# Last S5 layer: input product in float32, TensorE order written out, gate weight parts issued after the GELUs

## The chip, the cores and the metric

The kernel runs on one core of one Trainium2 chip. The metric is the device time of one execution, in microseconds, as the median of several runs. The engines are named as in the profile: PE is TensorE (matmuls and transposes), PEld its weight loads, DVE is VectorE, ACT is ScalarE, POOL is GpSimd, SP is SyncE. SP, ACT and POOL also issue DMA transfers, each in the order of its own queue.

## The reference

A residual trunk of four layers over 256 tokens of width 1024, all in float32. Each layer has a token mixer (layers 0 and 3 are S5, layer 1 is an attention, layer 2 a gated linear attention), a squared-ReLU MLP and a gated per-layer embedding. The change touches the S5 mixer of layer 3 alone:

```python
def s5_mixer(xn, w_in, ...):
    u = xn @ w_in                                  # 256 x 1024 times 1024 x 1024
    # per group of 16 channels: 64 complex states, a decayed scan over time
    x_re, x_im = einsum(u_blk, bbar_re), einsum(u_blk, bbar_im)
    s_re, s_im = associative_scan(...)             # in chunks of the sequence
    y = einsum(s_re, c_re) - einsum(s_im, c_im) + d_skip * u
    z1, z2 = split(gelu(y) @ w_glu, 2)             # 1024 x 2048
    return (z1 * sigmoid(z2)) @ w_out              # 1024 x 1024
...
h = h + s5_mixer(rmsnorm(h), ...)
...
h = h + (p[i] @ W_pp) * sigmoid(rmsnorm(h) @ W_pg)
```

## The kernel before

Activations lie transposed in SBUF: four tiles of 128 x 2 x 256 hold the residual stream. Almost every dense product is made of float32r matmuls on split operands. `parts` (lines 174 to 185) takes a raw weight tile of 128 x 1024, lets ACT cast it to a high part `whi` (L179) and lets DVE subtract that from the raw tile to get a low part `wlo` (L181). `scaled` (L363, L364) does the same with the activations. `col` (L198 to L200) then issues three matmuls for each 128 x 128 block of weights: high by high, high by low, low by high. Layer 0's S5 does not do so for its input product: there (L1158) the raw float32 weights are multiplied with the float32 activations, one matmul instruction per block, which the trace shows as two records.

The S5 layer works on four blocks b of 256 channels. Its steps have one-letter names, and a string of such steps (`FIRST` for layer 0, `LATER` for layer 3) is the order in which they are recorded:

- `D` loads a 512 x 256 piece of `w_in`, `h` splits it, `w` multiplies it (two pieces per block; pieces 2b and 2b+1 belong to block b and to the first and second half of the inputs). `c` scales the activations and squares them, `n` and `z` make the norm's factor (L330, POOL's power at L341, L351).
- `u` (L1166, DVE) scales the product and starts eight small DMAs that rearrange it into the tile `U` (L984), half issued by SP and half by ACT.
- `f` and `q` fetch the matrices that were prepared earlier for this block (`kept`, by POOL's queue). The first one that `f` fetches, `win`, has one buffer for all blocks.
- `x` is the way into the states (L996, 64 records on PE, written to two PSUM banks `wk`), `s` and `e` are the scan on DVE (L1006 to L1030), `y` is the way out (L1042) and the GELU on ACT (L1051).
- `t` transposes the block on PE (L1058) and copies it on ACT (L1059), `g` subtracts for the low part on DVE (L1231).
- `P` and `p` load and multiply the embedding's projection for the end of the layer (L446, float32 as it is).
- `d` loads a tile of the gate's half of `w_glu`, `l` splits it, `a` and `b` multiply it for the two column blocks of the gate (24 matmuls of `col` for each block of channels), with the sigmoid (L1257) after the last.

After these steps come the other half of `w_glu` and `w_out` as ordinary dense products, which wait for nothing but weights.

A tracing layer then places the instructions: it keeps each engine's program in an order of its own choosing that respects the data and the buffers, and need not follow the string. `in_order(engine)` (line 113) adds dependences that fix an engine to the recorded order; `issue_after` puts instructions behind a given one. In the kernel before, layer 3's steps have neither. Raw weight tiles share three buffers, the high and low parts four each, and every transfer waits in its issuing queue until its buffer is free.

What ends before layer 3's input product can begin is the product of the embedding's gate of layer 2 (`ple_gate`), whose last eight tiles use all high and low buffers, and whose results go through DVE and ACT (L468 to L471) into the residual stream that the S5 layer reads.

Of the kernel before, what the change touches and what calls it, by code (L numbers as in the profile page):

```python
# [12 lines left out]
AF = mybir.ActivationFunctionType  # L13
# [4 lines left out]
T, D, FF, DEPTH = 256, 1024, 4096, 4  # L18
# [12 lines left out]
d2 d3 t1 f3 x3 p2 p3 s2 a0 e2 y2 g1 q3 l2 d4 l3 d5 t2 b0 s3 a1 b1 g2 l4 e3 y3 l5 d6 d7 a2 b2 l6 l7 t3 g3 a3 b3"""  # L31

# [28 lines left out]
class Trunk:  # L61
# [373 lines left out]
    def plain_ple_proj(self, l, raws):  # L435

        nc = self.nc
        out = self.pp_done[l] = []
        for raw in raws:
            t = self.t4("pp", (128, 2, 2, T))  # L440
            for i in range(2):
                ps = self.psum((128, 2, T))
                for n in range(2):
                    for k in range(2):
                        c = (2 * i + n) * 128
                        nc.tensor.matmul(ps[:, n], raw[:, k, c:c + 128], self.praw[:, k], start=k == 0, stop=k == 1)  # L446
                nc.scalar.copy(t[:, i], ps)
                out.append(t[:, i])
                yield
# [583 lines left out]
    def s5_outputs(self, U, terms, out, tm):  # L1033

        nc = self.nc

        py = self.psum((128, 8, 64), "mk")
        gs = [slice(g * 64, (g + 1) * 64) for g in range(2)]
        def add(x, w, start=False, stop=False):
            for p in range(8):  # L1040
                for g in range(2):
                    nc.tensor.matmul(py[gs[g], p, :], x[gs[g], p, :], w[gs[g], :, p] if w is not tm else w[gs[g], p], start=start and p == 0,  # L1042
                                     stop=stop and p == 7, skip_group_check=True)
# [7 lines left out]
        nc.scalar.activation(G, py.rearrange("x p (i c) -> x i p c", i=4), AF.Gelu_apprx_tanh)  # L1051
        return G

    def s5_turn_over(self, G, hi):
# [55 lines left out]
    def s5_start(self, l):  # L1110


        nc, A = self.nc, self.A
        j = l // 3
        first = self.kept is None
# [29 lines left out]
        def product(i, between):  # L1145
            b, i = i // 2, i % 2
            if i == 0:
                us[b] = self.psum((128, 2, T), "acc")
            ps = us[b]
            if first:  # L1150
                raw = halves[2 * b + i]
            else:
                hi, lo = units.pop(("h", 2 * b + i))
            for n in range(2):
                c = slice(n * 128, (n + 1) * 128)
                for k in range(4):
                    if first:
                        nc.tensor.matmul(ps[:, n], raw[:, k, c], x[4 * i + k], start=i == k == n == 0, stop=i == 1 and k == 3, skip_group_check=True)  # L1158
                    else:
# [100 lines left out]
        steps = dict(D=D, h=h, w=w, u=u, c=c, n=n, z=z, f=f, j=j_, q=q_, r=r, i=i, o=o, k=k, x=x_, s=s, e=e, y=y, t=t, g=g, P=P, p=p, d=d, l=ahead, a=lambda b: gate(0, b),  # L1260
                     b=lambda b: gate(1, b))

        def run(order):
# [2 lines left out]
            return gT, v.get("last")  # L1266

        self.sg = []
        if first:
            halves = [self.raw0] + [self.half(w_in, i) for i in range(1, 8)]  # L1270
            x = [self.t4("x", (128, 4, T), tag="x4") for _ in range(2)]
            x = [x[k // 4][:, k % 4] for k in range(8)]
            scalars, v["ms"] = self.s5_scalars(j), self.psum((128, 2))

            def scaled(k):
# [170 lines left out]
```

## Time and profile before

| | |
|---|---|
| median of 3 runs | 1442.95 us (1440.83 to 1443.87) |
| profiled execution | 1441.32 us, its span 1439.3 us |
| granted TensorE clock, mean | 0.993 |
| PE busy | 1396.7 us, 97% of the span |
| DVE, ACT, POOL busy | 1047.1, 719.5 and 100.6 us |
| HBM traffic | 174 GB/s over the span |

The profile comes from one execution, 1.63 us below the median; about 2.0 us of its time lie outside the span. Times in the text count from the start of the span. Matmuls overlap: a record of 0.28 us can be followed by the next after 0.12 us, so costs in a row are taken from starts to starts.

### The profile page before, as it was taken

What the parts mean: (1) busy time and instruction counts of PE and PEld (TensorE: products, weight loads), DVE (VectorE), ACT (ScalarE), POOL (GpSimd) and SP (SyncE); (2) the same over time, 40 slices, a digit from 0 to 9 for tenths busy, and PEclk for the clock granted to TensorE, in tenths of its full rate; (3) what the DMA queues carried; (4) which work ended last, traced back from release to release, by engine and by line L of the source; (5) the groups of instructions that cost most, each with busy time, mean ns of one, the idle gap of its engine ahead of it and who ended that gap; (6) DMA issues with size and microseconds to landing.
All of it is one profiled execution on the core that took longest, in us unless ns stands there. A gap on an engine that the chain in (4) does not pass through costs nothing.

```text
span 1439.3 us, 26706 instructions
## 1 busy us (share of the span) xinstructions
PE 1396.7 (97%) x10818; PEld 1261.1 (88%) x10818; DVE 1047.1 (73%) x1652; ACT 719.5 (50%) x1118; POOL 100.6 (7%) x167
## 2 busy tenths in 40 slices
PE   9989999999999999999999999999997899999997
PEld 8888988889999888889988598888997799888897
DVE  9885678776866688897667468787676946766765
ACT  3233565454654655455567355445462345545543
POOL 3000000010010000000004000000003100000020
PEclk9999999999999999999999999999999999999999
DMA  9443656657554456766555256566656546556651
GB/s 297 111 120 108 180 171 196 189 183 238 171 157 136 122 167 193 248 226 211 196 161 170 94 153 196 195 215 197 205 162 210 172 152 181 179 183 194 188 189 59
DMA packets 143227, 254.54 MB, mean 177 GB/s; under 512 B 21648, under 2 KB 32240, under 8 KB 143104
## 3 DMA queue, kind: packets, MB, share of 16 engines
q1 hardware_dynamic: 129856, 227.66, 51.0%
q0 software_dynamic: 7360, 23.73, 4.8%
q10 hardware_dynamic: 5888, 1.44, 0.5%
q8 instruction: 84, 1.38, 0.4%
q14 instruction: 39, 0.32, 0.1%
HBM read 242.15 MB, written 7.86 MB: 174 GB/s over the span
## 4 chain that ended last, share of the span: by engine, by line
PE 63%; DMA 2%; DVE 2%; ACT 2%; issue 0%; DVEq 0%; POOLq 0%; ACTq 0%; SPq 0%
PE wk L234 9%; PE acc L234 7%; PE wk L236 4%; PE wk L198 4%; PE wk L199 4%; PE wk L200 4%; PE acc L198 4%; PE acc L199 3%; PE acc L200 3%; PE acc L236 3%; PE mk L234 3%; PE po L234 2%; PE mk L236 1%; PE acc L259 1%; PE acc L258 1%; PE acc L260 1%
## 5 line engine op out<-in xcount | busy, mean ns | idle before, releaser
L181 DVE TENSOR_TENSOR wlo<-raw,whi 128x1024 fp32r<-128x1024 f32 x404 | 492.0, 1226 | 276.2 <-ACT whi L179 274.6
L179 ACT CAST whi<-raw 128x1024 fp32r<-128x1024 f32 x404 | 420.8, 1049 | 489.4 <-DMA raw<-mlp_w 73.9
L234 PE MATMUL wk<-x,whi 128*128 128x512 f32 x576 | 181.3, 396 | 1.1 <-DVE relu L245 1.1
L236 PEld LDWEIGHTS wk<-x,wlo 128*128 128x128 f32 x576 | 106.8, 188 | 23.4
L234 PE MATMUL acc<-s,whi 128*128 128x512 f32 x384 | 119.2, 395 | 0.0
L236 PE MATMUL wk<-x,wlo 128*128 128x256 f32 x576 | 112.9, 279 | 0.0
L198 PE MATMUL acc<-x,whi 128*128 128x256 f32 x352 | 99.8, 287 | 1.8 <-DVE u L1166 1.0
L200 PE MATMUL acc<-x,wlo 128*128 128x256 f32 x352 | 99.9, 286 | 0.8 <-DVE wlo L181 0.8
L199 PE MATMUL acc<-x,whi 128*128 128x256 f32 x352 | 99.4, 285 | 0.0
L234 PEld LDWEIGHTS wk<-x,whi 128*128 128x128 f32 x576 | 90.3, 189 | 3.6 <-DVE relu L245 1.4
L236 PEld LDWEIGHTS acc<-s,wlo 128*128 128x128 f32 x384 | 71.0, 188 | 16.1
L234 PE MATMUL mk<-x,whi 128*128 128x512 f32 x256 | 81.5, 395 | 0.5 <-ACT whi L179 0.5
L236 PE MATMUL acc<-s,wlo 128*128 128x256 f32 x384 | 75.4, 280 | 0.0
L200 PE MATMUL wk<-s,wlo 128*128 128x256 f32 x256 | 72.4, 283 | 0.0
L199 PE MATMUL wk<-s,whi 128*128 128x256 f32 x256 | 72.4, 283 | 0.0
L198 PE MATMUL wk<-s,whi 128*128 128x256 f32 x256 | 72.4, 283 | 0.0
L198 PEld LDWEIGHTS acc<-x,whi 128*128 128x128 f32 x352 | 66.9, 191 | 3.3 <-issue 1.8
L200 PEld LDWEIGHTS acc<-x,wlo 128*128 128x128 f32 x352 | 67.2, 191 | 1.6 <-DVE wlo L181 1.3
L199 PEld LDWEIGHTS acc<-x,whi 128*128 128x128 f32 x352 | 67.2, 192 | 0.2
L234 PE MATMUL po<-s,whi 128*128 128x512 f32 x192 | 60.3, 395 | 0.0
L234 PEld LDWEIGHTS acc<-s,whi 128*128 128x128 f32 x384 | 59.1, 188 | 0.9
L234 PE MATMUL wk<-s,whi 128*128 128x512 f32 x192 | 59.1, 395 | 0.0
(404 smaller groups left out, 3362.9 us busy)
## 6 DMA issues: line engine op xcount, KB each, us to landing
raw<-mlp_w SPq DMA_DIRECT2D x256, 512.0 KB, 4.1
raw<-s_w_glu SPq DMA_DIRECT2D x32, 512.0 KB, 4.2
raw<-ple_gate SPq DMA_DIRECT2D x32, 512.0 KB, 3.6
raw<-fox_w_in SPq DMA_DIRECT2D x24, 512.0 KB, 3.8
raw<-gla_w_in SPq DMA_DIRECT2D x24, 512.0 KB, 4.6
raw<-s_w_out SPq DMA_DIRECT2D x16, 512.0 KB, 3.4
kept<-kept POOLq DMA_DIRECT2D x12, 512.0 KB, 4.7
raw<-s_w_in SPq DMA_DIRECT2D x11, 512.0 KB, 4.2
```

Of the source, the lines that this page charges most:

```text
L179: nc.scalar.copy(hi, raw)
L181: self.last_lo = nc.vector.tensor_tensor(lo, raw, hi.bitcast(F32), ALU.subtract)
L198: mm(ps, hi, x[:, 0], start=first, stop=False, skip_group_check=True)
L199: mm(ps, hi, x[:, 1], start=False, stop=False, skip_group_check=True)
L200: self.last_mm = mm(ps, lo, x[:, 0], start=False, stop=last, skip_group_check=True)
L234: mm(ps[n], hi[:, i, s], v[i], start=first and i == 0, stop=False, skip_group_check=True)
L236: self.last_mm = mm(ps[n][:, 0], lo[:, i, s], v[i][:, 0], start=False, stop=last and i == UK - 1, skip_group_check=True)
L258: mm(ps[half], a[:, 0, t], hi[:, k], start=k0 + k == 0, stop=False)
L259: mm(ps[half], a[:, 0, t], lo[:, k], start=False, stop=False)
L260: mm(ps[half], a[:, 1, t], hi[:, k], start=False, stop=k0 + k == nk - 1)
```

## The change

Layer 3 now makes its input product as layer 0 does. `D` loads the raw pieces with `half`, which places them in turn in buffers of the raw, the high and the low parts; step `h` is gone; `c` scales the activations in ACT alone, without a low part; `w` issues 8 float32 matmul instructions per piece where 24 float32r ones stood. `LATER` is written anew, without the `h` steps, with the products `w` spread between the steps of the blocks and `t3` between two gate products. The layer's steps stand under `in_order` for PE. The splits of the gate's weights (`l`) are issued after the last GELU recorded so far. The other lines only hand references on.

```diff
-LATER = """D0 D1 D2 h0 D3 h1 D4 c0 w0 h2 D5 n0 z0 f0 q0 w1 h3 D6 z1 h4 D7 w2 w3 u0 h5 P0 u1 h6 d0 x0 w4 h7 d1 w5 f1 q1 s0 x1 u2 w6 e0 y0 w7 f2 t0 l0 P1 s1 x2 q2 u3 p0 p1 e1 y1 g0 l1
...
+LATER = """D0 D2 D1 D3 c0 w0 w2 n0 z0 f0 q0 w1 z1 D4 D5 u0 w3 P0 u1 w4 D6 D7 d0 x0 s0 w5 d1 f1 q1 x1 e0 w6 y0 u2 s1 w7 t0 l0 g0 f2 x2 u3 P1 e1 q2 y1 l1 d2
...
     def s5(self, l):
...
-        with nullcontext():
-            steps = self.s5_start(l)
-            with nullcontext():
-                gT, last = steps()
+        steps = self.s5_start(l)
+        with nullcontext() if l == 0 else self.in_order(E.PE):
+            gT, last = steps()
...
         def D(i):
-            units["h", i] = self.raw(w_in[i % 2 * 512:(i % 2 + 1) * 512, i // 2 * 256:(i // 2 + 1) * 256], 4, 256)
-
-        def h(i):
-            units["h", i] = self.parts(units["h", i])
+            units["h", i] = self.half(w_in, i)
...
                 for k in range(4):
-                    if first:
-                        nc.tensor.matmul(ps[:, n], raw[:, k, c], x[4 * i + k], start=i == k == n == 0, stop=i == 1 and k == 3, skip_group_check=True)
-                    else:
-                        self.col(ps[:, n], v["x"][2 * i + k // 2][:, k % 2], hi[:, k, c], lo[:, k, c], i == k == n == 0, i == 1 and k == 3)
+                    self.last_mm = nc.tensor.matmul(ps[:, n], raw[:, k, c], x[4 * i + k], start=i == k == n == 0, stop=i == 1 and k == 3, skip_group_check=True)
...
         def c(_):
-            v["x"] = self.scaled(l)
+            for k in range(8):
+                nc.scalar.activation(x[k], self.H[k], AF.Identity, scale=self.gains[:, l, k:k + 1])
             v["sq"] = self.squares()
...
         def ahead(i):
-            units[i % 2, i // 2] = self.parts(units[i % 2, i // 2])
+
+            with nullcontext() if first else self.tc.issue_after(self.last_gelu.ins):
+                units[i % 2, i // 2] = self.parts(units[i % 2, i // 2])
```

On PE, in the middle of layer 3's S5 stretch, the difference of the two programs reads as follows. L996 is the way in, L1042 the way out, L1150 the input product (L1158 before).

```order
-L996 MATMUL wk<-U,kept 64x64 x16
-L1042 MATMUL mk<-tm_108,U 64x64 x5
-L996 MATMUL wk<-U,kept 64x64 x16
-L1042 MATMUL mk<-tm_108,U 64x64 x11
+L1150 MATMUL acc<-x,raw 128x256 x8
+L1150 MATMUL acc<-x,wh 128x256 x8
 L996 MATMUL wk<-U,kept 64x64 x32
+L1150 MATMUL acc<-x,wl 128x256 x8
+L996 MATMUL wk<-U,kept 64x64 x32
+L1150 MATMUL acc<-x,raw 128x256 x8
+L1042 MATMUL mk<-tm_108,U 64x64 x16
 L1042 MATMUL mk<-kept,P 64x64 x32
```

Before, no input product stood between the ways in of blocks 0 and 1 and the way out of block 0; now the pieces 3 to 6 stand there one by one, and piece 7 behind the way out.

On DVE, before, from the start of block 0's scan (P_11790, W_11791 and R_11789 are block 0's tiles; u_11832 is the third block's input):

```order
L1006 TENSOR_TENSOR P_11790<-wk_11687,kept_11548 128x1024
L1006 TENSOR_TENSOR W_11791<-wk_11704,kept_11548 128x1024
L1166 TENSOR_TENSOR u_11832<-acc_11721,rstd_11594 128x2x64x4
L1007 TENSOR_TENSOR R_11789<-P_11790,W_11791 128x512
L1008 TENSOR_TENSOR R_11789<-P_11790,W_11791 128x512
L1011 SCALAR_TENSOR_TENSOR R_11789<-decay_11550,R_11789 128x512
L181 TENSOR_TENSOR wlo_12102<-raw_11750,whi_12101 128x1024
```

The same engine in the changed kernel, from the end of block 0's chain (W_11630) through block 1's (P_11771, W_11772, R_11770) to the third block's input u_11759:

```order
L1028 TENSOR_TENSOR W_11630<-R_11628,kept_11515 128x16x63
L1006 TENSOR_TENSOR P_11771<-wk_11660,kept_11649 128x1024
L1006 TENSOR_TENSOR W_11772<-wk_11677,kept_11649 128x1024
L1029 TENSOR_TENSOR P_11629<-P_11629,W_11630 128x8x63
L1030 TENSOR_TENSOR P_11629<-P_11629,W_11630 128x8x63
L1007 TENSOR_TENSOR R_11770<-P_11771,W_11772 128x512
L1008 TENSOR_TENSOR R_11770<-P_11771,W_11772 128x512
L1011 SCALAR_TENSOR_TENSOR R_11770<-decay_11651,R_11770 128x512 x2
L1019 MEMSET P_11771 128x16
L1021 TENSOR_TENSOR P_11771<-R_11770,kept_11649 128x16x63
L1028 TENSOR_TENSOR W_11772<-R_11770,kept_11649 128x16x63
L1156 TENSOR_TENSOR u_11759<-acc_11579,rstd_11539 128x2x64x4
```

The third block's input moved from behind the first two instructions of block 0's chain to behind nearly the whole of block 1's.

On SP, the transfers of this stretch in the changed kernel:

```order
L269 DMA raw<-s_w_in 128x4x256 x2
L171 DMA raw<-ple_proj 128x2x512
L269 DMA wl<-s_w_in 128x4x256
L269 DMA wh<-s_w_in 128x4x256 x2
L269 DMA wl<-s_w_in 128x4x256
L269 DMA wh<-s_w_in 128x4x256
L269 DMA raw<-s_w_in 128x4x256
L984 DMA U<-u 128x1x64 x8
L171 DMA raw<-s_w_glu 128x2x512 x2
L984 DMA U<-u 128x1x64 x4
L171 DMA raw<-ple_proj 128x2x512
L984 DMA U<-u 128x1x64 x4
```

Before, eight raw pieces, both tiles of `ple_proj` and two of `s_w_glu` stood ahead of the first U transfers; now one tile of `ple_proj` and no `s_w_glu` do.

More of the change, by code (lines that the diff above doesn't have):

```diff
@@ L445, in plain_ple_proj @@
                         c = (2 * i + n) * 128
-                        nc.tensor.matmul(ps[:, n], raw[:, k, c:c + 128], self.praw[:, k], start=k == 0, stop=k == 1)
+                        self.last_mm = nc.tensor.matmul(ps[:, n], raw[:, k, c:c + 128], self.praw[:, k], start=k == 0, stop=k == 1)
                 nc.scalar.copy(t[:, i], ps)
@@ L1050, in s5_outputs @@
         G = self.t2("G", (128, 4, 8, 16))
-        nc.scalar.activation(G, py.rearrange("x p (i c) -> x i p c", i=4), AF.Gelu_apprx_tanh)
+        self.last_gelu = nc.scalar.activation(G, py.rearrange("x p (i c) -> x i p c", i=4), AF.Gelu_apprx_tanh)
         return G
@@ L1149, in product @@
             ps = us[b]
-            if first:
-                raw = halves[2 * b + i]
-            else:
-                hi, lo = units.pop(("h", 2 * b + i))
+            raw = units.pop(("h", 2 * b + i))
             for n in range(2):
@@ L1258, in gate @@
                 self.sg.append(sg)
-        steps = dict(D=D, h=h, w=w, u=u, c=c, n=n, z=z, f=f, j=j_, q=q_, r=r, i=i, o=o, k=k, x=x_, s=s, e=e, y=y, t=t, g=g, P=P, p=p, d=d, l=ahead, a=lambda b: gate(0, b),
+        steps = dict(D=D, w=w, u=u, c=c, n=n, z=z, f=f, j=j_, q=q_, r=r, i=i, o=o, k=k, x=x_, s=s, e=e, y=y, t=t, g=g, P=P, p=p, d=d, l=ahead, a=lambda b: gate(0, b),
                      b=lambda b: gate(1, b))
@@ L1268, in s5_start @@
         self.sg = []
+        x = [self.t4("x", (128, 4, T), tag="x4") for _ in range(2)]
+        x = [x[k // 4][:, k % 4] for k in range(8)]
         if first:
-            halves = [self.raw0] + [self.half(w_in, i) for i in range(1, 8)]
-            x = [self.t4("x", (128, 4, T), tag="x4") for _ in range(2)]
-            x = [x[k // 4][:, k % 4] for k in range(8)]
+            units["h", 0] = self.raw0
+            for i in range(1, 8):
+                D(i)
             scalars, v["ms"] = self.s5_scalars(j), self.psum((128, 2))
```

4 lines of the change are left out of this document (1 added, 3 removed).

## The prediction

> **What bounds the kernel now.** I read the page first, then busy time by stretch, then what PE waits for, then rows in order of time around layer 3's S5 part.
>
> ```profile
> span 1439.3 us, 26706 instructions
> PE 1396.7 (97%) x10818; PEld 1261.1 (88%) x10818; DVE 1047.1 (73%) x1652; ACT 719.5 (50%) x1118; POOL 100.6 (7%) x167
> ```
>
> PE is busy 97% of the span, so time comes back only where PE is idle or slow, and any matmul time added where PE is full is paid. The stretches of layer 3's S5 part (columns: length; busy time of PE, PEld, DVE, ACT, POOL; granted clock; DMA share; GB/s):
>
> ```profile
> 1074.15:1100.70 26.55, 24.95 (x204) 24.34 (x202) 16.45 (x24) 12.50 (x20) 5.21 (x9) 1.00 0.70 220
> 1100.70:1130.00 29.30, 16.70 (x318) 15.34 (x318) 26.20 (x30) 7.45 (x11) 8.99 (x16) 0.86 0.70 223
> 1130.00:1172.60 42.60, 41.54 (x563) 39.13 (x562) 27.42 (x31) 16.03 (x22) 2.84 (x5) 0.97 0.38 120
> 1172.60:1195.90 23.30, 23.30 (x197) 23.30 (x196) 12.76 (x13) 9.93 (x11) 0.00 (x0) 1.00 0.61 194
> ```
>
> The first is the input product, the second the scans, the third the gate, the fourth plain dense product without a gap. In the second PE is busy 16.70 of 29.30 us while DVE is busy 26.20. PE's waits from 1066 to 1230 us, all of them:
>
> ```profile
> PE wk L446 <- DVE P L1006: 4.7, 1, 4.7
> PE wk L996 <- issue: 3.7, 1, 3.7
> PE mk L1042 <- DVE P L1029: 3.6, 1, 3.6
> PE acc L198 <- ACT g L1059: 1.1, 1, 1.1
> PE acc L198 <- DVE u L1166: 1.0, 1, 1.0
> PE wk L996 <- DMA U<-u: 0.7, 1, 0.7
> PE acc L200 <- DVE wlo L181: 0.6, 1, 0.6
> ```
>
> They sum to 15.4 us; three of them make 12.0. Each of the three has an aftermath (PE alone, then the clock):
>
> ```profile
> 1108.20:1111.90 3.70, 3.67 (x64) 0.54 0.99 321
> 1115.46:1118.90 3.44, 3.44 (x70) 0.55 0.96 383
> 1128.84:1132.50 3.66, 3.66 (x10) 0.54 0.50 155
> ```
>
> Behind each idle of 3.6 us or more the clock is about half for about 3.6 us, which loses about 1.65 us each time, 5.0 in all. So the stretch holds 20.4 us that are not work.
>
> **The change part by part.**
>
> *The product in float32.* Layer 0 has the same shapes, raw by raw; beside it, two high products of `col` one block apart, and the layer's start and end marks:
>
> ```profile
> 23.11 3.72 PE L1158 MATMUL acc<-x,wl 128*128 128x256 f32 x16
> 26.67 3.62 PE L1158 MATMUL acc<-x,raw 128*128 128x256 f32 x16
> 1154.77 0.28 PE L198 MATMUL wk<-g,whi 128*128 128x256 f32 x1
> 1155.13 0.28 PE L198 MATMUL wk<-g,whi 128*128 128x256 f32 x1
> 1074.15 0.28 PE L198 MATMUL acc<-x,whi 128*128 128x256 f32 x1
> 1195.89 0.28 PE L198 MATMUL acc<-glu,whi 128*128 128x256 f32 x1
> ```
>
> A piece of 8 instructions (16 records) takes 26.67 - 23.11 = 3.56 us; the same piece split takes 8 x 0.36 = 2.88. Eight pieces: 28.5 instead of 23.0, so **+5.4 us of PE work**, all on the path. What leaves: eight casts on ACT, eight `wlo` and eight low parts of x on DVE. In the first stretch these were mostly hidden behind PE (idle there: 0.6 and 1.0 us), so by themselves they pay about 1.6.
>
> *The order.* The gain must come from pieces standing where PE idled. I follow PE's new program with durations of the old one: 96 records of way out 2.94, four transposes 0.6 without their tail, an L446 group of 8 records 1.85 (half of the two in a row), a way in 2.1 (64 records; 32 take 1.15 with their tail).
>
> ```profile
> 1144.17 2.94 PE mk L1042 x96
> 1119.89 0.66 PE L1058 MATMUL po<-ident,G 128*128 128x128 f32 x4
> 1137.59 3.72 PE L446 MATMUL wk<-praw,raw 128*128 128x256 f32 x16
> 1087.79 0.79 PE wk L330 x8
> 1092.47 0.60 PE L351 MATMUL wk<-diag,ones 128*128 128x256 f32 x2
> 1093.58 1.94 DVE L1166 TENSOR_TENSOR u<-acc,rstd 128x512 f32<-128x512 f32 x2
> 1094.63 6.64 DMA U<-u
> 1106.85 4.89 DMA U<-u
> 1102.70 1.15 PE L996 MATMUL wk<-U,kept 64*64 64x64 f32 x31
> 1104.15 1.64 POOL L1125 DMA_DIRECT2D kept<-kept  x3 [10.62 <-PE wk L996]
> 1108.20 3.67 PE L996 MATMUL wk<-U,kept 64*64 64x64 f32 x64 [3.65 <-issue]
> ```
>
> PE starts w0 at 1074.15 as before (its x, the first half, is scaled before that; its raw piece came early). w0, w2: 1081.3. Means 0.8, w1: 1085.65. L351 and w3, w4: 1093.0. From L351's start the old trace needs 2.1 us to the end of the first `u` (1092.47 to half of 1093.58 + 1.94), so here u0 ends at 1087.75. U then takes 4.89 or 6.64 us. Before, the 6.64 had a `ple_proj` tile and two gate tiles right ahead of it in the queue; now these are behind, so I take 4.89: U is there at 1092.65, before PE wants it. The 6.64 would add 1.5 us to all that follows.
>
> Way in 0: 1093.0 to 1095.1. w5: 1098.7. Way in 1 needs the next `win`, whose one buffer is free only when way in 0 ends: the old rows give 1103.85 to 1108.20, 4.35 us, so 1099.45, a **stall of 0.75**. The old stall of 3.65 is this same wait; w5 now covers the rest. Way in 1 to 1101.55, w6 to 1105.1, first part of way out 0 to 1106.1.
>
> DVE's chain for one block:
>
> ```profile
> 1127.57 1.21 DVE L1006 TENSOR_TENSOR P<-wk,kept 128x1024 f32<-128x1024 f32 x1
> 1128.70 0.68 DVE L1231 TENSOR_TENSOR g<-po,g 128x512 fp32r<-128x512 f32 x1
> 1135.25 1.20 DVE L1028 TENSOR_TENSOR W<-R,kept 128x1008 f32<-128x1008 f32 x1
> 1136.48 0.68 DVE L1029 TENSOR_TENSOR P<-P,W 128x504 f32<-128x504 f32 x1
> 1137.68 1.22 DVE L1006 TENSOR_TENSOR P<-wk,kept 128x1024 f32<-128x1024 f32 x1
> 1105.77 1.05 DVE L1166 TENSOR_TENSOR u<-acc,rstd 128x512 f32<-128x512 f32 x1
> ```
>
> From P to the end of L1028 8.3 us (without `g`'s 0.6), L1029 and L1030 1.2 more. Block 0 starts when the first bank is written, 1094.2: L1028 ends at 1102.5, block 1's P and W at 1104.8, L1029 and L1030 of block 0 at 1106.0. PE arrives at 1106.1: **the old 3.6 us wait is gone**, covered by w5 and w6. Way out 0 to 1108.1, w7 to 1111.7, t0 to 1112.3.
>
> What is late next is the third block's U. Its `u` had stood behind block 0's first two instructions; now it stands behind block 1's L1028, which ends at 1106.0 + 5.9 = 1111.9. `u` ends at 1112.85, U arrives at 1117.75. PE, in its fixed order, waits at way in 2 from 1112.3: a **new stall of 5.45 us**, and, as behind the old stalls, half clock: 3.67 for the way in instead of 2.1, 1.6 more, to 1121.4. By then the eight pieces are used up. Here the rows on the clock have no idle between 1.1 and 3.6 us. The Trainium skill (TensorE: Matmul & The Clock Gate, Part 1: The HAM clock gate) sets the halving at an idle window of about 3.4 us, free-running; by it a gap under that would spare the 1.6. The skill (DMA: Bandwidth & Descriptors, Anatomy of one DMA) gives a transfer about 2.0 us of fixed cost, so U would come about half a microsecond sooner than by the row if the issues take 2.4; an estimate, and the trace's 4.89 stands.
>
> From 1121.4 PE has 2.94 (way out 1), 3.7 (two L446 groups), 0.6, 2.1 (way in 3), 1.85, 2.94, 1.85, then gate products of 24 x 0.12 = 2.88 with the rest between: eight of them 23.0, two transposes 1.2, one way out 2.94: 43.2 us, to **1164.6**. The 4.7 us wait of L446 for a `wk` bank goes: the bank is read by block 2's P at about 1121, and L446's second group comes at about 1126. Block 2's chain ends at about 1131 and way out 2 wants it at about 1133; block 3's ends at about 1141 against 1149.
>
> *Gate parts behind the GELUs.* On ACT the cast of the third tile waits for GELU 2 (way out 2 ends about 1135.5): cast about 1137.3, `wlo` behind block 3's chain about 1142.2; wanted at 1143.7. The last two casts wait for GELU 3 (about 1153): `wlo` about 1156.5, wanted at 1158.7 and 1161.6. **Cost nothing, with 1.5 to 2 us of cover**; if that cover goes, a gate product waits for as long as it is late. t3 stands two products ahead of its user, so the old 1.1 us wait for `g` goes.
>
> *Five pieces in the high and low buffers.* They load when the gate of layer 2 lets go of them, from about 1065 to 1071 us, and are wanted from 1077.7 on, at 4.2 us each: no cost.
>
> **The sum.** Before, the fourth stretch's end less its 64 x 0.36 = 23.04 gives a start of plain dense work at 1172.85; now 1164.6: 8.25 us less. My old account does not close by 1.2 us: the work before, by the same durations with pieces of 2.88, is 77.1, the loss 20.4, and the length 98.7. Such crumbs remain, so I take **7.0 us less**: 21.6 lost before, about 9 after (0.75 + 5.45 + 1.6 + 1.2), 5.4 work added. Against the profiled 1441.32 it gives 1434.3; that execution was 1.6 below the median, so **1436.0** for the median of 1442.95.
>
> **The rivals.**
>
> *U and its wait are longer.* U takes 6.64 at both places and the crumbs double: 1.5 + 1.75 + 1.2: the gain is 2.5, 1440.5. For it: the DMA engines are 70% busy in both old stretches. Against it: fewer tiles ahead in the queue.
>
> *The third gap closes.* If U is there when PE comes, 5.45 + 1.6 more are gained: 1429. For it: every U transfer but the first is small. Against it: DVE's order is fixed by the program, and its chain alone ends at 1111.9.
>
> *No gain.* The fixed order turns short waits, which the old order filled with whatever was ready, into as many new ones: 5.4 of work plus 7 us of such waits, about 1443. For it: PE's program before does mix records of several steps (9 of L1042 inside a way in); against it: it did not help there, 12 us of waits remained.
>
> *Slower: the gate's weights set the pace.* Three raw buffers serve P, the gate and the next weights, and tiles are let go only after cast and `wlo`. If each tile then follows the one before at its landing time of 4.2 us instead of PE's 2.88, the eight gate products take 8 x 1.3 = 10.6 more:
>
> ```profile
> raw<-s_w_glu SPq DMA_DIRECT2D x32, 512.0 KB, 4.2
> ```
>
> That gives 1446.6; it decides from 3.75 us per tile on, where it eats the 7.0. Against it: the fourth stretch runs the same kind of tiles at full PE with a DMA share of 0.61.
>
> **How the numbers follow.** My forecast (1432 to 1438.5) 0.55; the longer wait 0.18, about two thirds of it on the faster side; the closed gap 0.10; no gain 0.11; slower 0.06. What a measurement can tell from no change is 0.2%, 2.9 us. Faster by more: 0.55 + 0.12 + 0.10 = 0.77; same 0.06 and all but 0.01 of the no gain, 0.16; slower the rest, 0.07. The range leaves out most of the closed gap, half of the no gain and the slower case: 1431 to 1442.5.
>
> **What would show it.** In the new profile: pieces of 3.5 to 3.6 us; the waits of L1042 for L1029 and of L446 for P gone; the wait ahead of way in 1 under 1.5 us; one long wait of 4 to 7 us at way in 2 for U with the clock near 0.54 behind it; plain dense work starting about 8 us sooner. It is wrong if other waits above 2 us stand between the gate products, if way in 0 waits, or if a gap beyond way in 2 halves the clock.

## The result and the profile after

| | before | changed |
|---|---|---|
| median | 1443.41 us (4 runs, 1440.83 to 1444.47) | 1432.41 us (4 runs, 1428.31 to 1433.93) |
| profiled execution | 1441.32 us | 1428.31 us, the fastest of the four |
| layer 3's S5 stretch, first input product to first product of `w_out` | 121.74 us | 111.96 us |

The ratio is 0.9928, with a 95% interval of 0.9912 to 0.9944: 10.4 us faster (8.1 to 12.7). Executions of one kernel differ by some 2 us either way in places that no edit touches, so below each run is given by its ratio and by the length of its stretch in the one execution that was profiled. The stretch goes by the prediction's two marks; the expectations call its end the first plain dense product, but it is the row `acc<-glu`, and the last 23.04 us ahead of it (64 x 0.36) are the plain product with the other half of `w_glu`.

The page of the changed kernel, span and engines:

```profile
span 1426.6 us, 26530 instructions
PE 1396.1 (98%) x10754; PEld 1258.1 (88%) x10754; DVE 1034.8 (73%) x1636; ACT 710.6 (50%) x1110; POOL 100.6 (7%) x167
```

PE's busy time is the same as before (1396.7); the span is 12.7 us shorter. The whole stretch by window, before and then after (columns as in the prediction: length; busy time of PE, PEld, DVE, ACT, POOL; granted clock; DMA share; GB/s):

```profile
1074.15:1195.89 121.74, 106.48 (x1277) 102.10 (x1276) 82.82 (x97) 45.91 (x64) 17.04 (x30) 0.96 0.57 181
```

```profile
1071.17:1183.13 111.96, 107.10 (x1213) 100.14 (x1211) 75.89 (x87) 39.81 (x59) 17.02 (x30) 0.98 0.59 185
```

9.8 us of the difference lie here; the remaining 2.9 lie ahead of it and are the difference of two executions: in the second profile of this kernel, below, the stretch begins at 1072.82 and not at 1071.17. PE's idle time in the stretch went from 15.3 to 4.9 us, although PE's work grew. All waits of PE from 1066 to 1230 us after the change:

```profile
PE wk L996 <- issue: 3.0, 1, 3.0
PE mk L1042 <- issue: 1.3, 1, 1.3
PE wk L996 <- DMA U<-u: 0.6, 1, 0.6
PE wk L330 <- DVE relu L245: 0.5, 1, 0.5
```

The two waits for DVE (4.7 and 3.6), the 1.1 for `g` and the 0.6 for `wlo` are gone. What is left in the stretch stands at the ways in of blocks 1 and 2, and 1.3 us inside way out 1. Of the pieces, 3 and 4 stand right ahead of way in 0, piece 5 between the ways in of blocks 0 and 1, piece 6 behind way in 1 and piece 7 behind way out 0. PE's rows there, in order of time (start, length, instruction, idle time ahead of it):

```profile
1089.86 2.08 PE L996 MATMUL wk<-U,kept 64*64 64x64 f32 x64
1091.87 3.72 PE L1150 MATMUL acc<-x,wl 128*128 128x256 f32 x16
1098.61 2.57 PE L996 MATMUL wk<-U,kept 64*64 64x64 f32 x64 [3.03 <-issue]
...
1113.53 2.48 PE L996 MATMUL wk<-U,kept 64*64 64x64 f32 x64 [0.55 <-DMA U<-u]
```

Way in 0 does not wait; way in 1 waits 3.03 us, way in 2 only 0.55. The profile shows no data that the 1.3 us inside way out 1 waited for, and no later profile has this wait. The chain of waits has ahead of way in 2 the transfer of block 2's U:

```profile
1110.46 2.93 DMA U<-u
```

### The profile page after: what moved, and what is told of

Same layout as the page of the kernel before. It is cut to its first block, busy times and chain, and to the rows that moved or that the text cites. A ratio compares the mean times of both kernels' runs of the same rounds, so it can differ in the third digit from the quotient of the medians.

```text
span 1426.6 us, 26530 instructions
## 1 busy us (share of the span) xinstructions
PE 1396.1 (98%) x10754; PEld 1258.1 (88%) x10754; DVE 1034.8 (73%) x1636; ACT 710.6 (50%) x1110; POOL 100.6 (7%) x167
## 4 chain that ended last, share of the span: by engine, by line
PE 66%; DVE 1%; ACT 1%; issue 1%; DMA 0%; DVEq 0%; POOLq 0%; ACTq 0%
PE wk L234 9%; PE acc L234 7%; PE wk L236 4%; PE wk L198 4%; PE wk L200 4%; PE wk L199 4%; PE acc L236 4%; PE acc L198 3%; PE acc L199 3%; PE acc L200 3%; PE mk L234 3%; PE po L234 2%; PE acc L1150 1%; PE mk L236 1%; PE acc L259 1%; PE acc L258 1%
## 5 line engine op out<-in xcount | busy, mean ns | idle before, releaser
L181 DVE TENSOR_TENSOR wlo<-raw,whi 128x1024 fp32r<-128x1024 f32 x396 | 482.2, 1226 | 278.3 <-ACT whi L179 275.6
L179 ACT CAST whi<-raw 128x1024 fp32r<-128x1024 f32 x396 | 412.2, 1049 | 461.2 <-DMA raw<-mlp_w 69.1
L198 PE MATMUL acc<-x,whi 128*128 128x256 f32 x288 | 81.7, 287 | 0.8 <-ACT pp L432 0.8
L200 PE MATMUL acc<-x,wlo 128*128 128x256 f32 x288 | 82.2, 286 | 0.2 <-DVE wlo L181 0.2
L199 PE MATMUL acc<-x,whi 128*128 128x256 f32 x288 | 81.8, 285 | 0.0
L234 PE MATMUL acc<-x,whi 128*128 128x512 f32 x192 | 58.8, 396 | 0.0
L236 PEld LDWEIGHTS mk<-x,wlo 128*128 128x128 f32 x256 | 47.6, 188 | 10.3
L198 PEld LDWEIGHTS acc<-x,whi 128*128 128x128 f32 x288 | 54.8, 191 | 2.1 <-ACT pp L432 1.3
```

The costliest lines, as they stand in the source:

```text
L179: nc.scalar.copy(hi, raw)
L181: self.last_lo = nc.vector.tensor_tensor(lo, raw, hi.bitcast(F32), ALU.subtract)
L198: mm(ps, hi, x[:, 0], start=first, stop=False, skip_group_check=True)
L199: mm(ps, hi, x[:, 1], start=False, stop=False, skip_group_check=True)
L200: self.last_mm = mm(ps, lo, x[:, 0], start=False, stop=last, skip_group_check=True)
L234: mm(ps[n], hi[:, i, s], v[i], start=first and i == 0, stop=False, skip_group_check=True)
```

## The experiments

Stretch lengths are by the same two marks in each profile. Against the kernel before, as it ran on the same chip:

| run | edit to | ratio (95%) | stretch | PE's waits in it |
|---|---|---|---|---|
| e1_again | (changed kernel) | 0.9910 (0.9894 to 0.9925) | 111.5 | 3.8 |
| e2_win_own | changed | 0.9961 (0.9948 to 0.9973) | 117.0 | 8.3 |
| e3_u2_early | changed | 0.9916 (0.9902 to 0.9929) | 111.3 | 3.9 |
| e4_both | changed | 0.9923 (0.9909 to 0.9936) | 112.8 | 4.1 |
| e5_only_f32 | before | 0.9963 (0.9949 to 0.9978) | 121.9 | 11.8 |
| e6_before_order | before | 0.9985 (0.9974 to 0.9995) | 122.7 | 16.0 |
| e7_no_order | changed | 0.9945 (0.9931 to 0.9960) | 115.1 | 7.0 |
| e8_no_gelu | changed | 0.9969 (0.9958 to 0.9980) | 121.3 | 10.9 |
| e9_brake | changed | 0.9957 (0.9941 to 0.9973) | 117.8 | 9.3 |
| e10_tuned | changed | 0.9915 (0.9897 to 0.9932) | 111.1 | 4.5 |
| e11_old_string | changed | 0.9955 (0.9937 to 0.9973) | 116.3 | 6.9 |
| e12_best | changed | 0.9904 (0.9888 to 0.9921) | 108.3 | 2.1 |

**The changed kernel again, no edit.**

> The changed kernel once more, for a second profile. My theory: the two waits of PE at the ways in of blocks 1 and 2 are one account. Block 2's U is ready at a time that DVE's chain sets (about 42.3 us after the layer's first input product begins), so what PE does not lose at way in 1 it loses at way in 2. Time again 1431 to 1434 us, the stretch from the first input product to the first plain dense product within 0.7 us of 112.0; the wait at way in 1 between 0.7 and 3.2 us by how long the load of win takes (4.4 to 6.4 us), and the wait at way in 2 correspondingly 0.5 to 4. Rival: the 3.0 us at way in 1 were an accident of one execution. Then it is under 1 us here, way in 2 waits about 5 us with half clock behind it, and the stretch is 2 to 3 us longer.

Measured: 1429.57 us, stretch 111.45. PE's waits:

```profile
PE wk L996 <- issue: 2.5, 1, 2.5
PE wk L996 <- DMA U<-u: 1.3, 2, 1.0
```

Way in 1 waits 2.55 us again, and way in 2 0.34 (the 1.0 is at way in 3). The wait at way in 1 belongs to the kernel, the rival falls.

**Buffers of its own for `win`.**

```diff
-                win = fetch(b, 0, (128, 2, 8, 64), "win")
+                win = fetch(b, 0, (128, 2, 8, 64), "wt")
```

> win gets buffers of its own for each block (a kind of tile that is free in layer 3), nothing else edited; the scheduler then puts block 2's u on DVE behind the last two instructions of block 1's chain, 1.2 us later. My theory (one account): the wait at way in 1 (3.0 us) and the half clock behind it (1.6) go, PE comes to way in 2 at 1108.4 on the clock of the first profile of the changed kernel, but u ends at about 1111.1 and U lands 2.9 to 4.9 us later, so way in 2 waits 5.6 to 7.6 us and has the half clock instead: 0.5 to 4 us SLOWER than the changed kernel, 1433 to 1436 us. Rival (the single buffer of win is the cause of a loss of its own): 4.6 us faster than the changed kernel, about 1428.

Measured: 1436.47 us, with a stretch 5.6 us longer than in the run without an edit. Slower, as my theory said and more so. PE's waits are now all of one kind:

```profile
PE wk L996 <- DMA U<-u: 8.3, 4, 5.5
```

Way in 2 by window, with half clock:

```profile
1121.55:1125.24 3.69, 3.65 (x70) 3.46 (x72) 1.34 (x2) 0.22 (x1) 0.00 (x0) 0.56 0.62 151
```

5.5 of the 8.3 stand at way in 2, just under the 5.6 to 7.6 that the account asked for. The other 2.8 I had not expected: they are at way **0**. The reason is on POOL's queue and on the DMA engines. POOL's issues in the changed kernel, in order of time:

```profile
1079.99 1.66 POOL L1124 DMA_DIRECT2D kept<-kept  x3
1081.64 2.33 POOL L961 DMA_DIRECT2D tm<-kept  x4
1092.24 1.64 POOL L1124 DMA_DIRECT2D kept<-kept  x3 [8.28 <-PE wk L996]
```

Its window from the norm's last product to way in 0, and from the view of tile U how long the transfers of U0 took from issue to landing (the profile has the landing of two of the eight):

```profile
1082.86:1089.86 7.00, 7.00 (x34) 5.89 (x32) 2.11 (x2) 0.37 (x1) 1.11 (x2) 1.00 0.71 244
```

```profile
DMA to landing us min/median/max: 2.4/2.5/2.6
```

The same three views of this run:

```profile
1082.60 1.67 POOL L1124 DMA_DIRECT2D kept<-kept  x3
1084.26 2.33 POOL L961 DMA_DIRECT2D tm<-kept  x4
1086.58 1.11 POOL L1124 DMA_DIRECT2D kept<-kept  x2
```

```profile
1085.46:1094.10 8.64, 7.07 (x33) 5.92 (x32) 2.11 (x2) 0.37 (x1) 6.41 (x12) 1.00 1.03 353
```

```profile
DMA to landing us min/median/max: 7.4/7.4/7.4
```

In the changed kernel block 1's loads wait in POOL's queue until way in 0 lets go of `win` (the 8.28 us). With more buffers they start at 1086.58, just ahead of U0's issues, the DMA engines are full (1.03 instead of 0.71), and U0's transfers take 7.4 us instead of about 2.5. The single buffer was a brake that kept the engines free for U. The new buffers are also another place in SBUF, and this run alone does not tell the two apart.

**Block 2's `u` early.** `u2` recorded ahead of block 0's rotation:

```diff
-... w5 d1 f1 q1 x1 e0 w6 y0 u2 s1 w7 ...
+... w5 d1 f1 q1 u2 x1 e0 w6 y0 s1 w7 ...
```

> Block 2's u is recorded ahead of block 0's rotation, so DVE does it inside block 0's chain, about 13 us sooner. win has one buffer as in the change. My theory: way in 2's wait of 0.55 us goes and nothing else, since way in 1 still waits for win (2 to 3 us with half clock): 0 to 1 us faster than the changed kernel, 1431.4 to 1432.4. Rival (DVE's order is what costs in the change, as the prediction said with 5.45 + 1.6 us): 3 us or more faster, 1429 or less.

Measured: 1430.19 us, stretch 111.34.

```profile
PE wk L996 <- DMA U<-u: 2.3, 3, 1.7
```

Way in 2 does not wait any more and the whole is the same: my theory holds. Way in 1 waited 1.57 this time, at full clock, but way in 3 waited 2.3 in three pieces: block 3's U (8.67 us in the chain of waits) went out together with block 3's matrices. POOL issued these three loads from 1114.49 on, U3 followed at 1115.06, and the two landings of U3 in the profile are:

```profile
DMA to landing us min/median/max: 7.6/8.1/8.7
```

`win` has its one buffer here, so the company of large loads is enough to slow U, without another place for `win`.

**Both.**

> Both edits: buffers of its own for win, and block 2's u early. My theory: only together do they give the account back: 3.0 (way in 1) + 1.6 (half clock) + 0.55 (way in 2) = 5.2 us faster than the changed kernel, about 1427.2 us; no new wait at way out 1, since block 1's chain on DVE ends at about 1111.1 and PE wants it at 1111.7 on the clock of the first profile. Rival (another wait takes their place at once, way out 1 behind DVE's chain): under 2 us faster, 1430.5 or more, with a wait of PE on DVE's L1030 of 3 us or more.

Measured: 1431.81 us, stretch 112.83, no gain. Both theories fall: way in 1 and way out 1 wait for nothing, but the rival's wait behind DVE did not come either. What came is the wait at way in 0 of the run with own buffers (2.7 us and some half clock), and 1.0 for a GELU.

**Float32 alone.** The kernel before with `half` and the raw product, the old string less its `h`, and neither `in_order` nor the rule for the gate's parts.

> The kernel before with only the product changed: float32 pieces without the split, the old string of steps less its splits h, no fixed order, no rule for the gate's parts. My theory (the product costs 5.4 us of PE and buys only room for the order): 5.4 added, less 1 to 2 us of idle time in the first stretch that the splits caused: 3 to 6 us SLOWER than before, 1445.5 to 1448.5, with the old waits for DVE's L1029 and L1006 still there. Rival (the splits on DVE and ACT were what delayed the scans): faster than before by 2 us or more, 1440 or less, the waits for DVE gone.

Measured: 1439.47 us, 3.2 to 7.4 us faster than before. My theory falls: the 5.4 us of PE work were paid back and more. From the first product to way in 0 it takes 25.2 us, with 6.9 of the eight longer pieces in them and no wait; before it took 27.3 with the eight shorter ones. The rival's mechanism fails too: DVE's waits are still there.

```profile
PE po L1058 <- ACT G L1051: 4.8, 1, 4.8
PE mk L1042 <- DVE P L1029: 3.7, 1, 3.7
PE wk L446 <- DVE P L1006: 2.2, 1, 2.2
```

Its profiled execution was the slowest of its five and has the stretch of before, so where the rest of the gain lies can't be read from it. It does show what takes the gain back there: when the wait for P ends, PE is 5.8 us ahead of the kernel before (48.9 us from the first product against 54.7), and then it waits 4.8 us for a GELU. On ACT a cast that waits for a tile of the gate's weights stands ahead of that GELU:

```profile
1131.88 1.04 ACT L179 CAST whi<-raw 128x1024 fp32r<-128x1024 f32 x1 [7.68 <-DMA raw<-s_w_glu]
1132.84 0.58 ACT L447 COPY pp<-wk 128x512 f32<-128x512 f32 x1
1133.31 0.60 ACT L1051 ACTIVATE G<-mk 128x512 f32<-128x512 f32 x1
```

**The order alone.** The kernel before with `in_order` for PE and the old string, the split product kept.

> The kernel before with only its TensorE order fixed for layer 3: the old string as it is written, split product kept, no rule for the gate's parts. The old string too has pieces between the steps of the blocks (w4, w5 between the ways in of blocks 0 and 1, w6 ahead of way out 0, w7 behind it), so by my theory (it is the pieces at these places that fill PE's waits) most of the gain is had without float32 and without its 5.4 us: 4 to 9 us faster than before, 1433 to 1438. Rival (the splits that float32 removes stand in the way: wlo of pieces 5 to 7 and of the gate's tiles now falls into DVE's chains and PE, in fixed order, waits for it): no gain or a loss, 1441 to 1448, with waits of PE for wlo or for DVE's chain of 3 us or more.

Measured: 1441.37 us, 0.7 to 3.7 us faster, though not in the profiled stretch, which is 1.0 us longer than before. The rival is the nearer one. PE waits right after the first piece:

```profile
PE wk L330 <- DVE sq L317: 6.8, 1, 6.8
PE po L1058 <- ACT G L1051: 3.5, 3, 2.2
```

In the old string the norm stands behind the first piece, and the squares for it stand behind the casts and low parts on ACT and DVE. Without a fixed order PE takes other pieces first (before, L330 starts 13.6 us after the first product); with it, PE waits 6.8 us. It is the old string that puts the norm there; in the run with the old string and float32, below, the same wait is 2.8, so the splits account for 4 us of it.

**Without the fixed order.**

```diff
-        with nullcontext() if l == 0 else self.in_order(E.PE):
+        with nullcontext():
```

> The changed kernel without the fixed order: float32, the new string, the rule for the gate's parts. The scheduler then draws the pieces together ahead of way in 0 and way in 1 (six of the eight before way in 0). My theory (the order is what gains): the gain goes: way in 1 waits about 3.7 us for win again and way out 0 for DVE's chain 3 to 4 us, each with half clock: 8 to 14 us slower than the changed kernel, 1439 to 1445. Rival (the new string and the free DVE gain, not the fixed order): within 3 us of the changed kernel, 1428 to 1434.

Measured: 1436.29 us, stretch 115.07, 3.1 to 3.6 longer than with it. Between the two theories. The pieces are drawn together as I said, but way in 1 does not wait and way out 0 waits 0.8 and not 3 to 4; the largest wait is the one that the prediction had put into the changed kernel, at way in 2 for block 2's U:

```profile
PE wk L996 <- DMA U<-u: 4.1, 1, 4.1
```

**Without the rule for the gate's parts.**

```diff
-            with nullcontext() if first else self.tc.issue_after(self.last_gelu.ins):
+            with nullcontext():
```

> The changed kernel without the rule that puts the gate's splits behind the GELUs. The scheduler then puts one or two wlo (1.2 us each) inside DVE's chains of blocks 1 and 2, two casts ahead of GELUs, and on SP a gate tile between the transfers of U3. My theory (the rule costs nothing and saves little): block 1's chain and with it U2 come 1.2 to 2.4 us later, way in 2 waits as much longer: 1 to 4 us slower than the changed kernel, 1431 to 1434. Rival (the rule does nothing, its cover is ample both ways): within 1 us of the changed kernel. A second rival (without it the gate's parts stop PE's scans outright, since a cast waits for a raw tile on ACT ahead of the U transfers): more than 5 us slower, 1435 or more.

Measured: 1439.66 us, stretch 121.28: 9.3 to 9.8 longer in the slowest of its eight executions, 6 to 8.5 us by the ratios: the second rival holds in its size and in its cast, though what PE waits for is the GELU and not U. PE's waits:

```profile
PE po L1058 <- ACT G L1051: 7.7, 2, 5.0
PE wk L996 <- issue: 3.2, 1, 3.2
```

ACT's longest wait from 1095 to 1140 us, and two of its rows in order of time:

```profile
ACT whi L179 <- DMA raw<-s_w_glu: 27.1, 3, 14.9
```

```profile
1133.34 1.04 ACT L179 CAST whi<-raw 128x1024 fp32r<-128x1024 f32 x1 [7.89 <-DMA raw<-s_w_glu]
1134.29 0.59 ACT L1051 ACTIVATE G<-mk 128x512 f32<-128x512 f32 x1
```

A cast stands ahead of the GELU on ACT and waits for a tile of the gate's weights that is still to land; the GELU, whose input is there, waits behind it, and PE, whose order is fixed, waits for the GELU at the transposes of blocks 0 and 1. The `wlo` in DVE's chains, which my theory went by, is not what costs.

**A brake at the start of way in.** Own buffers for `win`, and the next load recorded as to be issued after the first instruction of the way in before:

```diff
-                win = fetch(b, 0, (128, 2, 8, 64), "win")
+                with self.tc.issue_after(self.way_in.ins) if b else nullcontext():
+                    win = fetch(b, 0, (128, 2, 8, 64), "wt")
```

> win has buffers of its own as in the run before that did so, but the load of the next block's win is issued only once the way in of the block before has begun (there it was issued as early as the queue let it, in the changed kernel when that way in had ended, 2.1 us later than here). My theory (the loss at way in 0 came from company on the DMA engines: with the one buffer the matrices of block 1 cannot load while block 0's U is under way): way in 0 waits under 0.5 us again and is at full clock; way in 1 waits 0 to 1.2 us, without the half clock; way in 2 then waits 3.5 to 4.5 us for block 2's U, with half clock, since that u still stands behind block 1's chain. Stretch from the first input product to the first plain dense product 111 to 114 us, whole time 1429.5 to 1433.5. Rival (it was not the company, the other buffers themselves or their place cost): way in 0 waits 2 us or more again and the stretch is about 117.

Measured: 1435.01 us, stretch 117.76. The edit did not do what it says. POOL's issue of block 1's first two tiles, and PE's first row of way in 0:

```profile
1084.59 1.17 POOL L1125 DMA_DIRECT2D kept<-kept  x2
```

```profile
1092.40 0.45 PE L996 MATMUL wk<-U,kept 64*64 64x64 f32 x8 [1.85 <-DMA U<-u]
```

The loads go out 7.8 us before way in 0 begins: `issue_after` did not make POOL wait for the way in. So this run repeats the one with own buffers and does not tell company from place.

**All together.** Own buffers with that brake, `u2` early, block 3's `u` ahead of `wlo`, the second tile of `ple_proj` behind block 3's U.

> All together: win in buffers of its own, loads of blocks 1 and 2 issued when the way in before begins, block 2's u early on DVE, block 3's u ahead of the wlo of the gate's first tile, and the second tile of ple_proj behind block 3's U on SP. My theory (DVE's chain sets a floor that lies below PE's own work once every U is early and alone on the DMA engines): the waits of PE ahead of the gate fall from 4 to 5 us to under 1.5 us and no half clock is left: stretch 106 to 108 us against 111.3 to 112.0, whole time 1424 to 1427. Rival (the transfers only collide elsewhere: the loads of block 3, which now start earlier, meet the U of block 2): way in 2 or way in 3 waits 2 us or more, 1428 or more.

Measured: 1429.91 us, stretch 111.07: my theory falls, the brake again not being one. Way in 0 waits 2.2 us in company as before; the other edits give back as much. The rival's time came, but not its waits: ways in 2 and 3 wait for nothing.

**The old string in the changed kernel.**

> The changed kernel with the old string of steps (less h): float32, fixed order and the rule for the gate's parts stay. It sets way in 0 behind four pieces instead of five with the norm one piece sooner, two pieces between the ways in of blocks 0 and 1, block 2's u earlier on DVE, the embedding's two products together, way out 2 behind the first gate product, and t3 right ahead of its user. My theory (of the change the three parts float32, fixed order and the rule gain, the new string little): way in 0 waits 1 to 3 us for U0, the ways in 1 and 2 less than in the changed kernel, t3's user 1.1 us for g: 0 to 4 us slower than the changed kernel, 1430 to 1434. Rival (the placing of the pieces in the new string is what gains): 5 us or more slower, 1435 or more, with waits of 3 us or more at way in 0 and ahead of way out 1 or way out 2.

Measured: 1436.08 us, stretch 116.29, 4.3 to 4.8 longer: nearer the rival in size, but by none of the waits that it named.

```profile
PE wk L330 <- DVE sq L317: 2.8, 1, 2.8
PE acc L198 <- ACT g L1059: 2.0, 1, 2.0
```

The norm behind one piece instead of two costs 2.8, with slow clock for the next piece; t3 right ahead of its user costs 2.0 and 0.3 for `g`; two transposes wait 0.7 each for a GELU. Way in 0 waits for nothing.

**The company kept away.** `win` in two tiles of one buffer each, so that the brake is a buffer again but the first half follows sooner and is half as large; `u2` early; block 3's `u` ahead of `wlo`; the second tile of `ple_proj` in a buffer of its own and loaded during the MLP before; the gate's first two tiles asked for later.

```diff
-                win = fetch(b, 0, (128, 2, 8, 64), "win")
-                ins[b] = [[win[:, i]] for i in range(2)]
+                win = [fetch(b, 0, (128, 8, 64), tag, i * 512) for i, tag in enumerate(("win", "bx"))]
+                ins[b] = [[t] for t in win]
...
-... D6 D7 d0 x0 s0 w5 d1 f1 q1 x1 e0 w6 y0 u2 s1 w7 t0 l0 g0 f2 x2 u3 P1 e1 ...
+... D6 D7 x0 s0 w5 f1 q1 u2 x1 d0 e0 w6 y0 s1 w7 d1 P1 t0 g0 f2 x2 u3 l0 e1 ...
```

> The changed kernel with four edits that keep the company away from U. win is held in two tiles of one buffer each (real and imaginary part), so that block 1's matrices still cannot load before way in 0 has read its own, but the first half may follow 1 us earlier and is half as long; block 2's u early on DVE; block 3's u ahead of the wlo of the gate's first tile; the second tile of ple_proj in a buffer of its own, loaded during the MLP before; the gate's first two tiles are asked for one step later. My theory (way in 0 needs the single buffer as a brake, and the waits at the ways in 1, 2 and 3 come from loads that start late or in U's company): way in 0 waits under 0.5 us, the ways in 1 to 3 under 1 us each, no half clock; the first gate product begins 55 to 58 us after the first input product (changed kernel 61.2 to 61.7), stretch 105.5 to 108.5 us, whole time 1424 to 1427.5, faster than both kernels. Rival (another wait takes the gain: PE now comes to the gate sooner than its tiles, at 4.2 us a tile): waits for wlo or for the gate's tiles of 3 us or more between the gate products, stretch 109 us or more, 1428 or more.

Measured: 1428.28 us (1428.03 to 1429.64), 14.3 us faster than the kernel before. PE's waits in the stretch:

```profile
PE wk L996 <- DMA U<-u: 1.6, 2, 1.2
...
PE wk L996 <- DVE P L1019: 0.3, 1, 0.3
PE mk L1042 <- DVE P L1029: 0.2, 1, 0.2
```

The whole stretch by window:

```profile
1074.27:1182.53 108.26, 106.12 (x1212) 98.97 (x1211) 75.38 (x87) 39.72 (x59) 19.24 (x34) 1.00 0.59 186
```

Way in 0 does not wait, ways in 1 and 2 at most 0.3, and the clock is full throughout. The stretch is 3.2 and 3.7 us shorter than in the two profiles of the changed kernel, inside what I expected; the first gate product begins 58.0 us after the first input product, at the edge of it. The whole time is 0.8 above the range, where the rival had put it, but none of the rival's waits between the gate products came. By the intervals of the ratios it is not told apart from the changed kernel's. Of the waits, 1.6 are left at way in 3, over the 1 us expected, where block 3's U (SP) and matrices (POOL) go out together:

```profile
1114.61 1.63 POOL L1124 DMA_DIRECT2D kept<-kept  x3 [0.37 <-PE wk L996]
```

```profile
1114.78 2.59 SPq L984 DMA_DIRECT2D U<-u  x4
```

With this brake way in 0 does not wait, as in every run with float32 pieces and the one buffer, and in all four runs with own buffers it waits 2.2 to 2.8 us. That the company of the loads does this, and not the place of `win`, rests on U3 in the run with `u2` early; no run has the new place alone.

## Why the prediction was right

**Direction and place** held: faster by 8.1 to 12.7 us against 7.0 forecast, the median 3.6 below the forecast and inside the range, and the old waits for DVE are gone. What did not hold is how the new losses and the gain divide. Two of the signs that the prediction named did not come: way in 1 waits 3.0 and 2.5 us and not under 1.5, and there is no wait of 4 to 7 us at way in 2.

The chain of steps from start to plain dense work gave 8.25 us less and the profile shows 9.8. Of the 1.5 between them, 2.5 are at the ways in 1 and 2 (forecast 7.8 with the clock, measured 5.3) and about 0.3 in the pieces; against them stands the 1.3 inside way out 1, which no step had. That leaves nothing for "crumbs", so the 1.2 taken away for them should have stayed. Two slips in the steps are small: L351 gets 0.2 us where its rows give 0.4, and a U of 6.64 us would have added 1.4 and not 1.5. The steps in turn:

- *Float32 pieces.* From 1071.17 to 1074.62 a piece takes 3.45 us, and others at full clock up to 3.56, the forecast. But the forecast priced the leaving splits at 1.6 us, so float32 alone should have cost time. The run with float32 alone is 3.2 to 7.4 us faster than before although it does the added work (at least 8 x (3.45 - 2.88) = 4.6), so by the ratio what leaves is worth about 8 us or more; by its one profile, of its slowest execution, it is worth about 4.4. That step was mis-sized: part of what the prediction credited to the order comes from the splits that leave. How much, these profiles don't settle.
- *Way in 0 at 18.9 us without a wait.* 18.7, no wait. That U0 would be in time was right for a wrong reason, and so luck: I went by the tiles ahead of it in SP's queue. With that queue unchanged and POOL's loads let loose, two of its pieces took 7.4 us instead of 2.4 and 2.6, and way in 0 waited 2.8. The 2.0 us of fixed cost that the prediction quotes is given in that section for transfers issued by GpSimd; U's are issued by SP and ACT.
- *Way in 1 waits 0.75.* Measured 3.03, 2.55 and, with `u2` early, 1.57. The cause, the one buffer of `win`, is right: with more buffers this wait is gone. The size was off because I took the load's time from the old rows, 4.35 us; here it takes 6.4, from POOL's issue at 1092.24 to 1098.61. That a gate tile which SP asked for 1.4 us earlier slows it is likely, but no run tried that alone. The clock behind the wait was slow too, which I had reckoned with only from 3.6 us on.
- *Way in 2 waits 5.45, and 1.6 more by half clock.* Measured 0.55 and 0.34. U took 2.93 and not 4.89, and PE came 3.6 us later than in my account, by the wait at way in 1 and the clock. The two steps are one account: block 2's U is ready when DVE's chain lets it, and what PE does not lose at way in 1 it loses at way in 2. Forecast for both with the clock 7.8; measured 5.3, of which the clock is 3.6 x 0.31 + 3.8 x 0.16 = 1.7. The prediction had not seen that the two hang together; that its error at one made up for its error at the other was luck on its side. When the wait at way in 1 was taken away by own buffers, 5.5 us with half clock stood at way in 2 (with that `u` 1.2 us later on DVE, and PE later by its wait at way in 0).
- *The waits for DVE's L1029 and L1006, and for `g` at t3* went, as said. Without the new string the last comes back as 2.0 + 0.3.
- *Gate parts behind the GELUs cost nothing.* True, no gate product waits. But the step asked only what the rule costs and never what its absence would. Without it casts that wait for weights stop GELUs, and more than half of the gain is gone: the rival "no gain", in which a fixed order makes new waits, comes about in good part.
- *The gate's weights at 4.2 us a tile* did not set the pace of the gate products in any run; no such product waits more than 0.5 us for a `wlo`.

Alone, float32 gains about 5 us (0.9963) and the order about 2 (0.9985), against 10 to 13 for the whole; taking away the fixed order, the new string or the rule costs 2.5 to 5, 4 to 6.5 and 6 to 8.5. I read this as follows: fixing the order pays when nothing that PE must now wait for stands behind a slow queue. Float32 takes casts and low parts off ACT and DVE, the string moves the norm behind two pieces, and the rule takes the casts from ahead of the GELUs. The waits in the runs without each part agree; the new string and the rule were not tried alone.

## What to carry to other kernels

A fixed order on one engine is a promise that every other queue keeps its appointments: before writing it out, list what stands ahead of each awaited instruction on its own engine, and move work that waits for memory (a cast of a weight tile) behind what is awaited. Before giving a tile a second buffer, ask what its wait holds back: here the single buffer kept 1.5 MB of loads off the DMA engines while a small transfer on the critical path went through. And when two waits follow each other on a chain that a third engine paces, price them as one sum.

## What was unexpected of the hardware

- **Small transfers took three times as long in company.** U0's pieces of 32 KB landed 2.4 and 2.6 us after their issue with a DMA share of 0.71, and 7.4 us with a share of 1.03, though the loads that filled the engines came from another queue. U3 in the run with `u2` early took 7.6 and 8.7 us at a mean share of 0.81, so the share alone does not set the time. The Trainium skill (DMA: Bandwidth & Descriptors, Issuing engines are not separate DMA queues) says that transfers started by different engines run on the same 16 DMA engines and interleave; the rows agree, and put 5 us on it here.
- **The clock fell after shorter idle times than before showed.** Behind the idle 3.03 us at way in 1:

```profile
1098.60:1102.20 3.60, 3.59 (x67) 3.30 (x68) 2.95 (x3) 0.00 (x0) 0.72 (x2) 0.69 0.27 106
1102.20:1106.00 3.80, 3.80 (x19) 2.97 (x19) 3.80 (x7) 0.00 (x0) 3.22 (x6) 0.84 0.86 279
```

In the second profile 2.55 us of idle time did the same (way in 1 took 2.81 us and the next piece 4.57), while 1.57 did not (2.08 and 3.72). Idle time in pieces gives both: 2.8 us in three pieces at way in 0 with own buffers was followed by half clock, 2.2 in two pieces in the run with all edits together was not. The slowing began 1.4 us into the work behind the wait and not at once, and then lasted about 3.3 us:

```profile
1098.61:1100.00 1.39, 1.39 (x47) 1.39 (x49) 0.88 (x2) 0.00 (x0) 0.00 (x0) 1.00 0.59 233
1100.00:1103.30 3.30, 3.30 (x29) 2.82 (x25) 3.16 (x4) 0.00 (x0) 1.82 (x4) 0.50 0.24 45
```

The Trainium skill (TensorE: Matmul & The Clock Gate, Part 1: The HAM clock gate) puts the drop at an idle window of about 3.4 us; here 2.55 us sufficed, and the measurement decides.
